# Head sums of an RWKV-7 preparation: one full product or four on the quarters of the array

## The chip, the cores and the metric

The kernel runs on one core of a Trainium2 chip. The metric is the device time of one execution in microseconds (us). The engines are called as in the profile: PE is TensorE (matmuls), PEld its weight loads, DVE VectorE, ACT ScalarE, POOL GpSimd, SP the queue that issues most DMAs. PE writes its results into eight PSUM banks of 128 partitions by 512 fp32 numbers.

## The reference

One decoder block on 512 tokens with a model width of 1024: a norm, one input projection, two mixers (sparse attention and RWKV-7), gates, an output projection, then a gated MLP with a short convolution. The change lies in the preparation of the RWKV-7 mixer, which has eight heads of 64 channels:

```python
r, k, v, a, decay = heads(r), heads(k), heads(v), heads(a), heads(decay)
kk = k * k_k
kk = kk / jnp.maximum(jnp.sqrt(jnp.sum(kk * kk, axis=-1, keepdims=True)), 1e-12)
k = k * (1.0 + (a - 1.0) * k_a)
...                        # the scan over tokens gives y, which is normalised per head
y = y + jnp.sum(r * k * r_k, axis=-1, keepdims=True) * v
```

Two sums over the 64 channels of a head occur for every token: the one of `kk * kk`, whose inverse root normalises the key, and the one of `r * k * r_k`, which weights the value.

## The kernel before

Activations are held with channels on the 128 partitions and the 512 tokens along the free dimension, so one tile holds two heads (a head pair, p = 0 to 3): head 0 in partitions 0 to 63, head 1 in 64 to 127. A projection (`dense_fm`) makes one such tile of 128 output channels from 24 matmuls of 512 columns: eight with the high part of the weights (`whi`) on each of two parts of the activations (`hh`, `hl`), eight with the low part (`wlo`). `wnext` loads the weights by DMA, one tile ahead of its use, and splits them in two on ACT and DVE.

The stage in question goes over the head pairs. For each, `front` makes the key `kx`, the rate `aa` and the decay (`cl`, `cum`, `ep`, `pi`; two products of 64 rows with `wa`, in banks "a" and "b"), `norms` the inverse root `rn`, `receptance` makes `rx`, `values_of` makes `vx`, `values_tok` turns `vx` to tokens on partitions (four transposes, L545) and copies it into `UV`, `vectors` makes the vectors of the state recurrence in a row of DVE operations and the term `BO`, and `gram` makes the 64x64 chunk matrices `AB` (transposes at L576, then products of 64 rows). The projections of the next pair are written between the steps of this one, so that PE has them while other engines work.

A sum over the channels of a head is a sum over 64 partitions. It is made by PE: `ones` is a 128x128 matrix with ones in two diagonal blocks of 64, and `mm(ss, ones, kk, True, True)` puts into all 64 partitions of a head the sum of that head, for 512 tokens. An fp32 product is carried out in two passes.

Order: in this stage it isn't written out by hand. Each engine's queue is in an order that the compiler's scheduler makes from the program's order (as priority), from dependencies and from its own estimate of times; `tc.high_priority()` raises a block's priority. Engines work through their queues in order. Later stages fix PE's order by hand (`manual_schedule`). PSUM banks come in three groups: "mm" (4 banks, for projections), "a" (2, from `pa()`) and "b" (2, from `pb()`). A new tile of a group waits until the oldest is read out. After the last pair, DVE inverts triangular blocks of `AB` in 31 steps, while PE does the projections of the attention.

Of the kernel before, what the change touches and what calls it, by code (L numbers as in the profile page):

```python
# [13 lines left out]
AF = mybir.ActivationFunctionType  # L14
ALU = mybir.AluOpType
# [8 lines left out]
DH = 64  # L24
H = 8
NH2 = H // 2
# [54 lines left out]
def hybrid_block(ctx: ExitStack, tc: tile.TileContext, A: dict, out: bass.AP):  # L81
# [25 lines left out]
    def bank(tag, bufs, shape=(128, 512)):  # L107
        return ps.tile(list(shape), F32, name="ps_" + tag, tag=tag, bufs=bufs)

    def mmb():  # L110
        return bank("mm", 4)

    def pa():
        return bank("a", 2)

    def pb():
        return bank("b", 2)

    def mm(o, l, r, start, stop):
        te.matmul(o, lhsT=l, rhs=r, start=start, stop=stop)  # L120

    def act(o, i, f=AF.Copy, **kw):
        sc.activation(o, i, f, **kw)  # L123

    def tt(o, a, b, op):
        v.tensor_tensor(o, a, b, op=op)  # L126

    def ts(o, a, s1, s2, op0=ALU.mult, op1=ALU.add):
        if s2 is None:
            v.tensor_scalar(o, a, s1, None, op0=op0)  # L130
        else:
            v.tensor_scalar(o, a, s1, s2, op0=op0, op1=op1)

    def stt(o, a, s, b, op0=ALU.mult, op1=ALU.add):
        v.scalar_tensor_tensor(o, a, s, b, op0=op0, op1=op1)  # L135
# [3 lines left out]
    ident, mask, ones, cmask = kc[:, 0:128], kc[:, 128:256], kc[:, 256:384], kc[:, 384:416]  # L139
# [16 lines left out]
    for name in ("rwkv_mu", "rwkv_w0", "rwkv_a0", "rwkv_k_k", "rwkv_k_a", "rwkv_r_k", "rwkv_ln_g", "rwkv_ln_b"):  # L156
        r0, n = ROWS[name]
        src = A[name]
        if name == "rwkv_r_k":
            src = src.rearrange("l h d -> l (h d)")  # L160
# [3 lines left out]
    pt = pa()  # L164
# [3 lines left out]
    def col(name, i=0):  # L168
        r0, n = ROWS[name]
        return prm[:, r0 + i:r0 + i + 1]  # L170
# [37 lines left out]
    def norm_tiles(pool_):  # L208
        return (cp.tile([128, NT, 2], F32, name="ss", tag="ss"),
                [pool_.tile([128, D], F32, name="h", tag="h", bufs=NT) for _ in range(NT)])  # L210
# [123 lines left out]
    with tc.manual_schedule(engines={getattr(mybir.EngineType, e) for e in ("PE", "Activation", "DVE", "Pool")}):  # L334
# [37 lines left out]
        for k in range(KT):  # L372
# [5 lines left out]
            if k == 6:  # L378
                pt = pa()
# [37 lines left out]
    def dense_fm(xh, xl, kt=KT):  # L417
        return run(dense_fm_g(xh, xl, kt))
# [12 lines left out]
    UV = rp.tile([128, NCH, NH2, 2, DH], F32, name="UV")  # L431
    BO = gp.tile([128, 4, S], F32, name="BO", tag="BO")
# [11 lines left out]
    def shift_mix(p, m, dst):  # L444
        mu = col("rwkv_mu", m)
        act(dst, p, AF.Copy, scale=omm[:, m:m + 1])
        stt(dst[:, 1:], p[:, :-1], mu, dst[:, 1:])

    def t2(name, bufs=1):
        return tp.tile([128, S], F32, name=name, tag=name, bufs=bufs)  # L450
# [11 lines left out]
    for name, (r0, n) in ROWS.items():  # L462
        if r0 >= NR0:
            r0 -= NR0
            src = A[name]
            if name.startswith("cmp_pe"):
                src = src.rearrange("l a d -> l (a d)")
# [10 lines left out]
    def chunks(ap):  # L478
        return ap.rearrange("p (c t) -> p c t", t=C)
# [15 lines left out]
    def front(p):  # L495
        cs = slice(128 * p, 128 * p + 128)
        kx = t2("kx", 2)
        pk = dense_fm(hh, hl)
        zw, za = pa(), pb()
        mm(zw, wa[0:64, cs], xw[0:64], True, True)  # L500
        mm(za, wa[64:128, cs], xw[64:128], True, True)
        shift_mix(pk, 4 + p, kx)
        cl = t2("cl")
        act(cl, zw, AF.Tanh, scale=0.5, bias=w0h[:, p:p + 1])
        aa = t2("aa", 2)
        act(aa, za, AF.Tanh, scale=0.5, bias=a0h[:, p:p + 1])
        ts(cl, cl, -0.5 * DECAY, -0.5 * DECAY)
        cum = t2("cum")
        v.tensor_tensor_scan(out=cum, data0=scanm.rearrange("p c t -> p (c t)"), data1=cl, initial=0.0,
                             op0=ALU.mult, op1=ALU.add)  # L510
        ep = tp.tile([128, NCH, C + 1], F32, name="ep", tag="ep", bufs=2)
        v.memset(ep[:, :, 0:1], 1.0)
        act(ep[:, :, 1:], chunks(cum), AF.Exp)
        pi = t2("pi", 2)
        act(pi, cum, AF.Exp, scale=-1.0)
        v.tensor_copy(PC[:, p, :, None], ep[:, :, C:C + 1])
        L[p] = dict(kx=kx, aa=aa, ep=ep, pi=pi)

    def norms(p):
        kx = L[p]["kx"]  # L520
        kk = t2("kk", 2)
        act(kk, kx, AF.Square, scale=col("rwkv_k_k", p))
        ss = pa()
        mm(ss, ones, kk, True, True)
        rn = t2("rn", 2)
        ts(rn, ss, 1e-24, None, op0=ALU.max)
        act(rn, rn, AF.Ln)
        act(rn, rn, AF.Exp, scale=-0.5)
        L[p].update(kk=kk, rn=rn)

    def receptance(p):
        rx = t2("rx", 2)
        shift_mix(dense_fm(hh, hl), p, rx)
        L[p]["rx"] = rx

    def values_of(p):
        vx = t2("vx")
        shift_mix(dense_fm(hh, hl), 8 + p, vx)
        L[p]["vx"] = vx

    def values_tok(p):
        vx = L[p]["vx"]
        pt = pb()
        for i in range(4):
            te.transpose(pt[:, 128 * i:128 * i + 128], vx[:, 128 * i:128 * i + 128], ident)  # L545
        for r in range(2):
            for cc in range(2):
                act(UV[64 - 64 * r:128 - 64 * r, cc::2, p, r, :],
                    pt[64 * cc:64 * cc + 64].rearrange("p (c r d) -> p c r d", r=2, d=DH)[:, :, r, :])

    def vectors(p):
        kx, aa, ep, pi, kk, rn, rx, vx = (L[p][k] for k in ("kx", "aa", "ep", "pi", "kk", "rn", "rx", "vx"))
        stt(AR[:, p, :, 1, :], chunks(rx), 1.0, ep[:, :, 1:], ALU.mult, ALU.mult)
        stt(kk, kx, col("rwkv_k_k", p), rn, ALU.mult, ALU.mult)
        stt(AR[:, p, :, 0, :], chunks(kk), -1.0, ep[:, :, 0:C], ALU.mult, ALU.mult)
        stt(kk, aa, 1.0, kk, ALU.add, ALU.mult)
        bh = tp.tile([128, NCH, 3, C], F32, name="bh", tag="bh")
        stt(bh[:, :, 0, :], chunks(kk), 0.5, chunks(pi), ALU.mult, ALU.mult)
        v.tensor_copy(bh[64:128, :, 2, :], bh[64:128, :, 0, :])
        ts(aa, aa, kah[:, p:p + 1], oma[:, p:p + 1])  # L560
        stt(kx, kx, 1.0, aa, ALU.mult, ALU.mult)
        stt(bh[:, :, 1, :], chunks(kx), 1.0, chunks(pi), ALU.mult, ALU.mult)
        tv = t2("tv")
        stt(tv, rx, col("rwkv_r_k", p), kx, ALU.mult, ALU.mult)
        L[p]["bh"] = bh
        bs = pa()
        mm(bs, ones, tv, True, True)
        tt(BO[:, p], bs, vx, ALU.mult)

    def gram(p):  # L570
        bh = L[p]["bh"]
        ptr = [pb(), pa()]
        for c in range(NCH):
            for r in range(2):
                rs = slice(64 * r, 64 * r + 64)
                te.transpose(ptr[r][:, 64 * c:64 * c + 64], bh[rs, c, r:r + 2].rearrange("p a t -> p (a t)"),  # L576
                             ident[rs, rs])
        for r in range(2):
            act(BKT[:, :, p, r, :], ptr[r].rearrange("p (c j) -> p c j", c=NCH))
        for c0 in range(0, NCH, 4):  # L580
            ptr = [mmb(), mmb()] if c0 else [pb(), pa()]
            for i in range(4):
                for r in range(2):
                    rs = slice(64 * r, 64 * r + 64)
                    mm(ptr[r][:, 128 * i:128 * i + 128], bh[rs, c0 + i, r:r + 2].rearrange("p a t -> p (a t)"),
                       AR[rs, p, c0 + i].rearrange("p a t -> p (a t)"), True, True)
            for r in range(2):
                tt(AB[:, c0:c0 + 4, p, r, :], ptr[r].rearrange("p (c t) -> p c t", c=4),
                   mask[:, None, :].to_broadcast([128, 4, 128]), ALU.mult)


    front(0)
    norms(0)
    receptance(0)
    values_of(0)
    late_params()
    for p in range(NH2):
        if p + 1 < NH2:
            front(p + 1)
            norms(p + 1)  # L600
        values_tok(p)
        vectors(p)
        if p + 1 < NH2:
            receptance(p + 1)
        gram(p)
        if p + 1 < NH2:
            values_of(p + 1)
        if p + 2 == NH2:
            kcp = dense_fm(hh, hl)
# [15 lines left out]
    for g in range(2):  # L625
        for b in range(2):
            r = 64 * g + 32 * b
# [75 lines left out]
    pt = pa()  # L703
# [31 lines left out]
    for b in (1, 0):  # L735
        for g in range(2):
            r = 64 * g + 32 * b
# [511 lines left out]
    for m in range(KT):  # L1249
        cs = slice(128 * m, 128 * m + 128)  # L1250
# [13 lines left out]
    ss, hs = norm_tiles(ntp)  # L1264
# [36 lines left out]
    with tc.manual_schedule(engines=KTS):  # L1301
        for t in range(NT):
            qs = slice(128 * t, 128 * t + 128)
            p = mmb()
# [13 lines left out]
        for pair in range(2):  # L1318
            cs = slice(256 * pair, 256 * pair + 256)
# [37 lines left out]
    for hf in range(2):  # L1357
        bo = dense_tok(512, aT[:, 0], aT[:, 1], NF)
        for t in range(NT):
            n = 256 if hf and t == NT - 1 else 512  # L1360
            for c0 in range(0, 512, n):
                cs = slice(512 * hf + c0, 512 * hf + c0 + n)
# [30 lines left out]
```

## Time and profile before

| | |
|---|---|
| median of 3 runs | 837.78 us (837.58 to 837.99) |
| the profiled execution | 837.93 us |
| its span, from the first to the last instruction | 836.1 us |
| granted clock of PE | 1.00 |
| the stage from front(0) to gram(3) | about 30 to 123 us of the span |

Times in the timelines count from the start of the span. A row gives start and duration in us, engine, line and operation; a line can be that of a helper: L120 is `mm`, L123 `act`, L126 `tt`, L130 and L132 `ts`, L135 `stt`, L299 the low part of a weight split. "x4" is a number of like instructions, and what stands in brackets is idle time of the engine before, and what ended it. A row of the groups gives after the count the busy us, the mean ns of one, and idle time before. PE's matmuls are pipelined, so their recorded durations overlap.

### The profile page before, as it was taken

What the parts mean: (1) busy time and instruction counts of PE and PEld (TensorE: products, weight loads), DVE (VectorE), ACT (ScalarE), POOL (GpSimd) and SP (SyncE); (2) the same over time, 40 slices, a digit from 0 to 9 for tenths busy, and PEclk for the clock granted to TensorE, in tenths of its full rate; (3) what the DMA queues carried; (4) which work ended last, traced back from release to release, by engine and by line L of the source; (5) the groups of instructions that cost most, each with busy time, mean ns of one, the idle gap of its engine ahead of it and who ended that gap; (6) DMA issues with size and microseconds to landing.
All of it is one profiled execution on the core that took longest, in us unless ns stands there. A gap on an engine that the chain in (4) does not pass through costs nothing.

```text
span 836.1 us, 12860 instructions
## 1 busy us (share of the span) xinstructions
PE 822.2 (98%) x5097; PEld 667.1 (80%) x5097; DVE 514.2 (62%) x998; ACT 406.7 (49%) x792; POOL 52.4 (6%) x69
## 2 busy tenths in 40 slices
PE   7999999999999999999999999999999999999998
PEld 5777778887787876777788988888888888888886
DVE  4478779973565778787664665666555666322222
ACT  6766654463555777676334454444444444221210
POOL 5200020140000100111000000000000000000000
PEclk9999999999999999999999999999999999999999
DMA  7432222346452310000275033332333332223421
GB/s 228 116 78 75 76 76 77 72 125 182 116 114 77 83 45 13 26 26 26 64 249 179 1 101 100 101 99 87 93 101 101 100 101 91 88 100 114 139 75 51
DMA packets 109104, 78.73 MB, mean 94 GB/s; under 512 B 3869, under 2 KB 97748, under 8 KB 109044
## 3 DMA queue, kind: packets, MB, share of 16 engines
q1 hardware_dynamic: 106512, 73.51, 30.4%
q10 hardware_dynamic: 1060, 2.55, 1.0%
q0 software_dynamic: 1472, 1.86, 1.0%
q8 instruction: 40, 0.66, 0.3%
q14 instruction: 20, 0.16, 0.1%
HBM read 74.56 MB, written 2.29 MB: 92 GB/s over the span
## 4 chain that ended last, share of the span: by engine, by line
PE 53%; DVE 0%; DVEq 0%; issue 0%
PE ps_mm L120 52%; PE ps_a L203 0%; PE ps_b L203 0%; PE ps_a L120 0%; PE ps_b L1197 0%; PE ps_mm L1197 0%; DVE x L126 0%; DVEq L1389 0%; PE ps_a L1149 0%
## 5 line engine op out<-in xcount | busy, mean ns | idle before, releaser
L299 DVE TENSOR_TENSOR wlo<-raw,whi 128x1024 fp32r<-128x1024 f32 (+1 forms) x111 | 131.5, 1186 | 184.8 <-PE ps_mm L120 157.2
L120 PE MATMUL ps_mm<-hh,whi 128*128 128x512 f32 (+1 forms) x624 | 242.6, 391 | 0.6 <-ACT whi L123 0.5
L120 PE MATMUL ps_mm<-hl,whi 128*128 128x512 f32 (+1 forms) x624 | 240.4, 387 | 0.0
L123 ACT ACTIVATE whi<-raw 128x1024 fp32r<-128x1024 f32 (+3 forms) x124 | 123.3, 996 | 165.2 <-PE ps_mm L120 143.9
L120 PE MATMUL ps_mm<-hh,wlo 128*128 128x512 f32 (+1 forms) x624 | 151.7, 384 | 0.0
L120 PEld LDWEIGHTS ps_mm<-hh,whi 128*128 128x128 f32 x624 | 117.3, 188 | 27.3 <-issue 1.3
L120 PEld LDWEIGHTS ps_mm<-hl,whi 128*128 128x128 f32 x624 | 117.4, 188 | 23.4 <-issue 1.0
L120 PEld LDWEIGHTS ps_mm<-hh,wlo 128*128 128x128 f32 x624 | 115.1, 188 | 23.3
L120 PE MATMUL ps_mm<-whi,aT 128*128 128x512 f32 x352 | 84.5, 390 | 0.0
L120 PEld LDWEIGHTS ps_mm<-whi,aT 128*128 128x128 f32 x352 | 65.9, 188 | 14.3 <-issue 0.4
L135 DVE SCALAR_TENSOR_TENSOR cgv<-ps_mm,cw,cgv 128x511 f32<-128x511 f32 (+1 forms) x88 | 65.4, 746 | 1.6
L123 ACT ACTIVATE cgv<-ps_mm,cw 128x512 f32<-128x512 f32 x44 | 34.2, 779 | 23.3 <-PE ps_mm L120 23.3
L120 PE MATMUL ps_mm<-wlo,aT 128*128 128x512 f32 x176 | 44.3, 389 | 0.0
L123 ACT ACTIVATE P<-P,nm 128x512 f32<-128x512 f32 (+3 forms) x64 | 35.3, 553 | 14.9 <-DVE nm L1171 14.9
L123 ACT ACTIVATE aT<-cgv 128x512 fp32r<-128x512 f32 x22 | 13.9, 632 | 56.8 <-DVE cgv L126 56.8
L120 PEld LDWEIGHTS ps_mm<-wlo,aT 128*128 128x128 f32 x176 | 33.0, 188 | 6.9
L123 ACT ACTIVATE cgv<-cgv 128x512 f32<-128x512 f32 x22 | 13.9, 632 | 41.0 <-DVE cgv L135 41.0
L299 POOL TENSOR_TENSOR wlo<-raw,whi 128x512 fp32r<-128x512 f32 (+3 forms) x13 | 20.5, 1573 | 202.2 <-PE ps_mm L120 148.2
L1171 DVE CUSTOM_DVE_ANT_0 P<-ps_a,AB 128x512 f32<-128x512 f32 (+3 forms) x64 | 29.4, 485 | 4.2 <-PE ps_a L120 3.7
L126 DVE TENSOR_TENSOR x<-x,ps_mm 128x512 f32<-128x512 f32 (+1 forms) x17 | 11.1, 655 | 23.6 <-PE ps_mm L120 22.0
L126 DVE TENSOR_TENSOR aT<-cgv,aT 128x512 fp32r<-128x512 f32 x22 | 15.2, 693 | 14.7 <-ACT aT L123 14.7
L120 PE MATMUL ps_a<-KH,qst 128*128 128x512 f32 (+3 forms) x64 | 21.3, 348 | 1.6 <-DVE nm L1171 0.9
(358 smaller groups left out, 1199.1 us busy)
## 6 DMA issues: line engine op xcount, KB each, us to landing
raw<-in_w_up_dram SPq DMA_DIRECT2D x44, 512.0 KB, 3.8
raw<-in_w_in_dram SPq DMA_DIRECT2D x38, 512.0 KB, 3.9
raw<-in_w_down_dram SPq DMA_DIRECT2D x22, 512.0 KB, 3.6
raw<-in_w_out_dram SPq DMA_DIRECT2D x8, 512.0 KB, 3.5
xt<-in_x_dram SPq DMA_DIRECT2D x4, 512.0 KB, 5.9
raw<-in_cmp_w_v_dram SPq DMA_DIRECT2D x4, 512.0 KB, 3.8
raw<-in_w_proj_b_dram SPq DMA_DIRECT2D x8, 256.0 KB, 2.7
raw<-in_w_proj_a_dram SPq DMA_DIRECT2D x8, 256.0 KB, 2.7
```

What stands on the lines that cost most here:

```text
L120: te.matmul(o, lhsT=l, rhs=r, start=start, stop=stop)
L123: sc.activation(o, i, f, **kw)
L126: v.tensor_tensor(o, a, b, op=op)
L135: v.scalar_tensor_tensor(o, a, s, b, op0=op0, op1=op1)
L299: eng.tensor_tensor(lo, raw, hi.bitcast(F32), op=ALU.subtract)
L1171: v.tensor_tensor_reduce(out=P[:, i], in0=sp[:, N * (i - i0):N * (i - i0) + N], in1=BT[:, h, 384 - 128 * qt:512], scale=-1.0, scalar=-NEG, ...
```

## The change

A head sum becomes four products of 64x64 with 256 tokens each (`head_sums`). For the first 256 tokens head 0's rows go to partitions 0 to 63 and head 1's to 64 to 127, into a bank "a"; for the other 256 tokens they go crosswise, into a bank "b". The four thus use the four quarters of the array, with two banks of which half is filled. What is read from bank "b" has its heads exchanged: `EXCH` lists the three pieces (the first 256 tokens whole, the others in two halves of 64 partitions), and the last step behind each sum undoes it, an Exp in three parts in `norms`, a multiplication in three parts in `vectors`. The clamp of `norms` is made in two parts and, like Ln, in `kk` in place of `rn`. Besides, `values_tok(p)` is written ahead of `norms(p + 1)`, and its four copies into `UV` get high priority.

```diff
+    def head_sums(src):
+        o = [pa(), pb()]
+        for i in range(2):
+            for r in range(2):
+                a, b = slice(64 * r, 64 * r + 64), slice(64 * (r ^ i), 64 * (r ^ i) + 64)
+                mm(o[i][b, 0:256], ones[a, a], src[a, 256 * i:256 * i + 256], True, True)
+        return o
+
+    EXCH = [(slice(0, 128), slice(0, 128), 0), (slice(0, 64), slice(64, 128), 1), (slice(64, 128), slice(0, 64), 1)]
+
     def norms(p):
         kx = L[p]["kx"]
         kk = t2("kk", 2)
         act(kk, kx, AF.Square, scale=col("rwkv_k_k", p))
-        ss = pa()
-        mm(ss, ones, kk, True, True)
+        ss = head_sums(kk)
         rn = t2("rn", 2)
-        ts(rn, ss, 1e-24, None, op0=ALU.max)
-        act(rn, rn, AF.Ln)
-        act(rn, rn, AF.Exp, scale=-0.5)
+        for i in range(2):
+            ts(kk[:, 256 * i:256 * i + 256], ss[i][:, 0:256], 1e-24, None, op0=ALU.max)
+        act(kk, kk, AF.Ln)
+        for d, s_, i in EXCH:
+            cs = slice(256 * i, 256 * i + 256)
+            act(rn[d, cs], kk[s_, cs], AF.Exp, scale=-0.5)
...
-        for r in range(2):
-            for cc in range(2):
-                act(UV[64 - 64 * r:128 - 64 * r, cc::2, p, r, :],
-                    pt[64 * cc:64 * cc + 64].rearrange("p (c r d) -> p c r d", r=2, d=DH)[:, :, r, :])
+        with tc.high_priority():
+            for r in range(2):
+                for cc in range(2):
+                    act(UV[64 - 64 * r:128 - 64 * r, cc::2, p, r, :],
+                        pt[64 * cc:64 * cc + 64].rearrange("p (c r d) -> p c r d", r=2, d=DH)[:, :, r, :])
...
-        bs = pa()
-        mm(bs, ones, tv, True, True)
-        tt(BO[:, p], bs, vx, ALU.mult)
+        bs = head_sums(tv)
+        for d, s_, i in EXCH:
+            cs = slice(256 * i, 256 * i + 256)
+            tt(BO[d, p, cs], bs[i][s_, 0:256], vx[d, cs], ALU.mult)
...
         if p + 1 < NH2:
             front(p + 1)
+        values_tok(p)
+        if p + 1 < NH2:
             norms(p + 1)
-        values_tok(p)
         vectors(p)
```

## The prediction

> **What bounds the kernel now.** I read the page first, then busy time by stretches over the stage that the change touches (from 30 us, front(0), to 123 us, the end of gram(3)), then the timelines of each engine there.
>
> ```profile
> span 836.1 us, 12860 instructions
> PE 822.2 (98%) x5097; PEld 667.1 (80%) x5097; DVE 514.2 (62%) x998; ACT 406.7 (49%) x792; POOL 52.4 (6%) x69
> ```
>
> The profiled execution took 837.93 us, so 1.83 us lie around its span; the median of the runs is 837.78, or 0.15 lower. TensorE (PE) is busy for 98% of the span, so time is won by taking work from PE, if no new wait takes its place, and lost by any stop of PE. Where a wait could come from shows in the stretches of one head pair. Their columns are busy us (instructions) of PE, weight loads, DVE, ACT and POOL:
>
> ```profile
> 74.60:85.00 10.40, 10.40 (x81) 8.03 (x82) 5.24 (x8) 10.00 (x16) 0.00 (x0) 1.00 0.36 99
> 85.00:95.40 10.40, 10.40 (x47) 8.58 (x48) 10.24 (x16) 3.79 (x5) 0.00 (x0) 1.00 0.18 51
> 97.08:107.50 10.42, 10.42 (x81) 8.05 (x82) 5.24 (x8) 10.03 (x16) 0.00 (x0) 1.00 0.36 101
> 107.51:118.67 11.16, 10.96 (x48) 8.71 (x47) 11.03 (x17) 3.76 (x5) 0.06 (x1) 1.00 0.13 45
> ```
>
> The averages (62% and 49%) hide this: in the first half of each period of 22.5 us ACT is 96% busy (from cl of front to rx of receptance), in the second DVE is 98 to 99% busy (from rx to vx of values_of). The two halves form one chain, cl to rx on ACT and then rx to vx on DVE, and its end is awaited by the four transposes at L545. How much room it has:
>
> ```profile
> 95.44 0.74 DVE L135 SCALAR_TENSOR_TENSOR vx<-ps_mm,prm,vx 128x511 f32<-128x511 f32 x1
> 96.98 0.66 PE L545 MATMUL ps_b<-kc,vx 128*128 128x128 f32 x4
> ...
> 117.93 0.74 DVE L135 SCALAR_TENSOR_TENSOR vx<-ps_mm,prm,vx 128x511 f32<-128x511 f32 x1
> 118.73 0.66 PE L545 MATMUL ps_b<-kc,vx 128*128 128x128 f32 x4 [0.26 <-DVE vx L135]
> ```
>
> For head pair 2 vx ends at 96.18, 0.80 us before PE comes to it. For head pair 3 there is no next front to cover it, and PE already waits: DVE sets the time there.
>
> **Head sums on PE.** Eight products are replaced: kk and tv, four times each. In the timeline of PE (start, duration, operation), the two of period 2:
>
> ```profile
> 99.56 1.02 PE L120 MATMUL ps_a<-kk,kc 128*128 128x512 f32 x2
> 100.42 1.02 PE L120 MATMUL ps_a<-tv,kc 128*128 128x512 f32 x2
> 100.88 0.79 PE L120 MATMUL ps_mm<-hl,whi 128*128 128x512 f32 x1
> 101.51 0.40 PE L120 MATMUL ps_mm<-hh,whi 128*128 128x512 f32 x1
> ```
>
> Durations include the latency of the pipeline, so I go by starts. From kk to tv are 0.86 us: two passes of 512 columns at 0.43. A dense matmul takes 0.226 (below), so the one before 101.51 took the array at 101.28, and tv also cost 0.86: a full product costs nothing for coming and going. The new form is four 64x64 products of 256 columns on the four quarters, two passes of 0.215 each. That four quarters with different streams do run together, the state loop shows, with U and the next chunk's own products on four quarters and two banks:
>
> ```profile
> 185.27 0.81 PE L120 MATMUL ps_mm<-wlo,hh 128*128 128x280 f32 x5
> 186.01 0.27 PE L120 MATMUL ps_b<-Xs,AB 64*64 64x64 f32 x2
> 186.03 0.27 PE L120 MATMUL ps_b<-UV,AB 64*64 64x64 f32 x2
> ...
> 186.48 0.23 PE L120 MATMUL ps_b<-UV,AB 64*64 64x64 f32 x2
> 186.64 0.40 PE L120 MATMUL ps_mm<-whi,hh 128*128 128x280 f32 x1
> 186.87 0.30 PE L120 MATMUL ps_mm<-whi,hl 128*128 128x280 f32 x1
> ```
>
> Two groups of two start 0.02 apart, and eight such steps are 0.064 apart, where 64 columns alone would be 0.43/8 = 0.054. But the block as a whole is dearer. The five before it step by (0.81 - 0.29)/4 = 0.13 and end their stream at 185.92; the dense work is back in step at 186.87 - 0.13 = 186.74. Of those 0.82 us the steps are 0.51; 0.31 goes to entering and leaving. The same from the pair of front, half the rows each:
>
> ```profile
> 29.62 1.97 PE L120 MATMUL ps_mm<-hh,wlo 128*128 128x512 f32 x8
> 31.53 0.69 PE L120 MATMUL ps_a<-xw,wa 64*128 64x512 f32 x1
> ...
> 32.06 0.59 PE L120 MATMUL ps_a<-xw,wa 64*128 64x512 f32 x1
> ...
> 32.59 0.50 PE L120 MATMUL ps_mm<-hh,whi 128*128 128x512 f32 x1
> 32.92 0.39 PE L120 MATMUL ps_mm<-hl,whi 128*128 128x512 f32 x1
> ```
>
> Dense steps are (1.97 - 0.39)/7 = 0.226, so the stream ends at 31.43 and is back at 32.69: 1.26 us for two passes of 0.43, 0.40 for the switch. I take 0.36, midway. The Trainium skill differs within itself here: TensorE: Matmul & The Clock Gate, Part 3, counts for a pack of small products the span of one plus some 4 ns for each further one and nothing for the switch, by which a head sum would cost 0.44 (an estimate) and the eight would win 3.4 us; TensorEngine Tiling, Key Properties, says that changing the tiling mode drains the engine. Both blocks here are with the second.
>
> A head sum by itself then costs 0.43 + 0.36 = 0.79 against 0.86: 0.07 won. Two in a row share the switch: 0.86 + 0.36 = 1.22 against 1.72, 0.50 won. In three periods kk of the next pair and tv of this one do stand together, as above, and I expect that to stay: they take their banks in the same order, and the transposed values are out of their bank earlier. Together: 0.07 for kk of pair 0, 3 x 0.50, and for tv of pair 3, which goes on to gram's own small products and pays one side only, 0.86 - 0.43 - 0.18 = 0.25. PE work falls by 1.8 us. If the order puts dense matmuls between the two, 0.36 is lost each time.
>
> **What it adds on ACT and DVE.** Half-width operations are dearer than half:
>
> ```profile
> L123 ACT ACTIVATE rn<-rn 128x512 f32<-128x512 f32 x8 | 5.1, 632 | 0.1
> L123 ACT ACTIVATE QK<-ps_mm 64x256 f32<-64x256 f32 x8 | 3.0, 376 | 0.7 <-PE ps_mm L120 0.6
> L126 DVE TENSOR_TENSOR BO<-ps_a,vx 128x512 f32<-128x512 f32 x4 | 2.8, 692 | 2.1 <-PE ps_a L120 2.1
> L126 DVE TENSOR_TENSOR sC<-sC,mx 128x256 f32<-128x256 f32 x8 | 3.4, 420 | 0.0
> ```
>
> The last Exp becomes three of about 0.376: 1.13 for 0.63, +0.50 in each period, in ACT's full half and ahead of rx in its queue. The clamp becomes two of 0.42 for one like BO's 0.69 (+0.15), BO three for one (+0.57); both fall in the half in which DVE is busy 5.2 of 10.4 us and cost nothing while it has those 5 us. Ln stays whole. The matrix `ones`, the tiles and every DMA stay as they are; no queue of SP or POOL is touched.
>
> The order of values_tok and norms(p+1) changes little on PE, where the transposes came first already (96.98 before 99.56). The high priority does change ACT: the four evacuations move ahead of aa and the square of kk, which wait for them.
>
> ```profile
> 98.24 0.72 ACT L123 ACTIVATE kk<-kx,prm 128x512 f32<-128x512 f32 x1
> ...
> 102.90 1.99 PE L120 MATMUL ps_mm<-hh,wlo 128*128 128x512 f32 x8
> ...
> 119.42 1.54 ACT L123 ACTIVATE UV<-ps_b 64x256 f32<-64x256 f32 x4 [1.66 <-PE ps_b L545]
> ```
>
> They take 1.54 us, so the square ends near 100.5 instead of 98.96, and the head sums move later inside the dense product of receptance, which runs until 104.7 (the eight of its last part, from 102.90) and covers that. ACT's sum of work is the same, as long as Ln finds its clamp done: the chain grows by the 0.50 alone. Bounds: 0 (if Exp is queued behind rx) and 2.0 (if the 1.54 comes back as idle ACT).
>
> **Where it comes due.** With PE 0.50 shorter and the chain 0.50 longer a period, the room of 0.80 for L545 becomes -0.2 in periods 1 and 2: a small stop each. Up to front(3) PE is ahead by 0.07 + 0.50 + 0.50 - 0.2 = 0.87; vx of pair 3 comes 0.87 - 0.50 = 0.37 earlier, and the third pair's 0.50 is spent waiting for it. Then the tail of pair 3:
>
> ```profile
> 119.22 1.02 PE L120 MATMUL ps_a<-tv,kc 128*128 128x512 f32 x2
> 120.17 0.27 PE L576 MATMUL ps_b<-kc,bh 64*128 64x64 f32 x1
> 120.28 0.69 DVE L126 TENSOR_TENSOR BO<-ps_a,vx 128x512 f32<-128x512 f32 x1 [1.61 <-PE ps_a L120]
> 121.02 0.37 PE L120 MATMUL ps_b<-AR,bh 64*128 64x128 f32 x1
> ```
>
> There are two "b" banks. Before, the transposed values held one and gram's transposes (L576) took the other at 120.17; gram's products then waited until the evacuation ended at 119.42 + 1.54 = 120.96. Now tv's sum holds the second, and L576 itself must wait for that evacuation (or for BO's third part, 0.2 later). The 0.6 us of L576, hidden in that wait before, come behind it. Sum at gram(3): -0.37 + 0.6 = +0.2 us. After it PE works through in step, and DVE's inverse starts from the same point. So 837.93 + 0.2 = 838.1 for a profiled execution, 838.0 as median: no change that can be told (0.2%, 1.7 us, is about what a measurement of this kernel can tell).
>
> **Rivals.** Two of them rest on these rows:
>
> ```profile
> 35.95 0.68 DVE L130 TENSOR_SCALAR rn<-ps_a 128x512 f32<-128x512 f32 x1
> 36.37 1.28 ACT L123 ACT_TABLE_LOAD   x1
> ...
> 113.07 0.69 ACT L123 ACTIVATE vx<-ps_mm,omm 128x512 f32<-128x512 f32 x1 [0.75 <-PE ps_mm L120]
> ```
>
> (1) The gain comes through, 0.20: the DVE queue gets vx of pair 3 before tv's work, or L576 finds a bank. Then all 1.8 us are won, 836.1. For: the input of vx was ready at 113.76, four us before DVE came to it at 117.93, and any new order may move it. Against: it stood last in each of the periods before.
>
> (2) The quarters switch for free, 0.08: 8 x (0.86 - 0.43) = 3.4 us, 834.4, if order and waits allow it. Against are the two switch prices above, 0.31 and 0.40, and the chain. It is the time that the rule of the Trainium skill's TensorE: Matmul & The Clock Gate, Part 3, above would give.
>
> (3) Slower, 0.25: ACT's half becomes the period. Place: Ln, behind clamp, sum and square, all pushed back 1.54 us by the evacuations; the chain grows by 2.0 instead of 0.5. It decides from 0.3 of growth a period (0.80 - 0.50 of PE's lead). L545 then stops PE for 2.0 - 0.3 = 1.7 once before front(3); lag there -1.07 + 1.7 = +0.6, vx at +2.6, tail +0.6: +3.2, 841. For: ACT has 0.4 us idle in that half. Against: Ln has a table load ahead of it that does not wait for its clamp (36.37, while the clamp ran until 36.63), 1.28 us of ACT work that takes up most of the 1.54. The Trainium skill (TensorEngine Tiling, PSUM Bottleneck) warns that tiling leaves PSUM evacuation as it was, which is this case.
>
> (4) The change doesn't do what it says, 0.02: the quarters run one after another, 8 x (1.72 + 0.36 - 0.86) less three shared switches, +8.7, 846.6. The state loop's rows speak against it.
>
> **How the numbers follow.** The forecast has 0.45. Faster by over 0.2% (below 836.1): rival 2, 0.12 of rival 1, whose price lies at that edge, and 0.04 of the forecast's scatter from a new order, 0.24. Slower (above 839.5): 0.22 of rival 3, rival 4 and 0.06 of scatter, 0.30. The range reaches down to rival 1 and up almost to rival 3's price: 836.0 to 840.8.
>
> **What would show it.** Right: pairs of four-quarter head sums of about 1.2 us from dense to dense, PE waiting on vx at L545 and on UV at L576 of pair 3, PE busy near 821. Wrong: head sums that cost 0.5 each, dense matmuls between kk's and tv's quarters, vx of pair 3 well before PE needs it, or PE stopped for over a microsecond a period at L545.

## The result

The changed kernel takes 839.68 us (median of 10 runs, 839.29 to 841.28) against 837.84 before (10 runs, 837.50 to 838.32). The ratio is 1.0025, with a 95% interval of 1.0016 to 1.0035: slower by 1.8 us, inside the predicted range and just past the 0.2% up to which the prediction spoke of no change. By the prediction's own line of 839.5 this is the slower outcome, which it gave 0.30; its centre, 838.0, was missed by 1.7. The page after (busy time, share of the span, instructions):

```profile
span 837.6 us, 12983 instructions
...
PE 821.5 (98%) x5145; PEld 667.0 (80%) x5145; DVE 516.8 (62%) x1010; ACT 409.9 (49%) x800; POOL 52.8 (6%) x69
```

PE is busy 0.7 us less, but the span is 1.5 us longer. The waits of PE from 28 to 126 us of the span (sum, times, longest) say why:

```profile
PE ps_b L559 <- DVE vx L135: 2.0, 3, 1.3
PE ps_a L120 <- ACT kk L123: 1.0, 3, 0.7
PE ps_b L592 <- ACT UV L123: 0.5, 1, 0.5
PE ps_mm L120 <- DVE AB L126: 0.2, 1, 0.2
```

L559 and L592 are L545 and L576 of before. The same view of before has 0.3 us for `vx` and 0.2 for `AB`, 0.5 in all; now it is 3.7. In PE's timeline (start, duration, what the idle time before waited for):

```profile
57.25 0.43 PE L120 MATMUL ps_a<-kk,kc 64*64 64x256 f32 x2 [0.69 <-ACT kk L123]
...
74.65 0.66 PE L559 MATMUL ps_b<-kc,vx 128*128 128x128 f32 x4 [0.31 <-DVE vx L135]
...
119.82 0.66 PE L559 MATMUL ps_b<-kc,vx 128*128 128x128 f32 x4 [1.34 <-DVE vx L135]
...
122.12 0.46 PE L592 MATMUL ps_b<-kc,bh 64*128 64x64 f32 x4 [0.53 <-ACT UV L123]
```

The last pair's transposes come at 119.82 instead of 118.73. The last 16 Gram products (`ps_mm<-AR`) come at 123.54 instead of 122.01, and that difference of 1.53 is the difference of the spans: the stages behind it are as long as before.

The stretches of the last period, cut as in the prediction (from the transposes to `rx`, from `rx` to the next transposes; columns as there):

```profile
97.24:106.55 9.31, 9.13 (x82) 6.99 (x84) 6.62 (x11) 7.82 (x14) 0.00 (x0) 1.00 0.42 113
106.56:119.82 13.26, 11.92 (x64) 9.55 (x60) 11.21 (x17) 6.42 (x9) 1.20 (x1) 1.00 0.14 41
```

DVE's half was 11.16 us long and 99% busy; now it is 13.26 us long and 85% busy (11.21 / 13.26). DVE has hardly more to do in it (11.21 us against 11.03); it stands still. Its timeline shows where:

```profile
106.56 0.75 DVE L135 SCALAR_TENSOR_TENSOR rx<-ps_mm,prm,rx 128x511 f32<-128x511 f32 x1 [0.15 <-ACT rx L123]
109.14 0.75 DVE L135 SCALAR_TENSOR_TENSOR kk<-kx,prm,rn 128x512 f32<-128x512 f32 x1 [1.84 <-ACT rn L123]
109.81 0.69 DVE L135 SCALAR_TENSOR_TENSOR AR<-rx,ep 128x512 f32<-128x512 f32 x1
...
119.03 0.74 DVE L135 SCALAR_TENSOR_TENSOR vx<-ps_mm,prm,vx 128x511 f32<-128x511 f32 x1
```

The normalised key waits 1.84 us for the inverse norm `rn`, and AR's receptance part and the masked Gram blocks, which need no `rn`, stand behind it in the queue. Before, in the same place:

```profile
107.51 0.75 DVE L135 SCALAR_TENSOR_TENSOR rx<-ps_mm,prm,rx 128x511 f32<-128x511 f32 x1 [1.31 <-ACT rx L123]
108.18 0.74 DVE L135 SCALAR_TENSOR_TENSOR kk<-kx,prm,rn 128x512 f32<-128x512 f32 x1
```

There the key followed `rx` at once. Why `rn` is late, ACT's timeline shows, first before, then after:

```profile
101.95 1.28 ACT L123 ACT_TABLE_LOAD   x1
103.24 0.63 ACT L123 ACTIVATE rn<-rn 128x512 f32<-128x512 f32 x1
...
106.13 0.63 ACT L123 ACTIVATE rn<-rn 128x512 f32<-128x512 f32 x1
```

```profile
101.66 0.71 ACT L123 ACTIVATE kk<-kx,prm 128x512 f32<-128x512 f32 x1
...
104.02 1.28 ACT L123 ACT_TABLE_LOAD   x1 [0.71 <-DVE kk L130]
105.31 0.63 ACT L123 ACTIVATE kk<-kk 128x512 f32<-128x512 f32 x1
...
107.83 1.27 ACT L123 ACTIVATE rn<-kk 128x256 f32<-128x256 f32 x3
```

The square starts at 101.66 (before: 98.24), the load of Ln's table now waits for the clamp, and Exp in three takes twice as long: `rn` is complete at 109.10 instead of 106.76.

### The profile page after: what moved, and what is told of

Same layout as the page of the kernel before. It is cut to its first block, busy times and chain, and to the rows that moved or that the text cites. A ratio compares the mean times of both kernels' runs of the same rounds, so it can differ in the third digit from the quotient of the medians.

```text
span 837.6 us, 12983 instructions
## 1 busy us (share of the span) xinstructions
PE 821.5 (98%) x5145; PEld 667.0 (80%) x5145; DVE 516.8 (62%) x1010; ACT 409.9 (49%) x800; POOL 52.8 (6%) x69
## 4 chain that ended last, share of the span: by engine, by line
PE 53%; DVE 0%; DVEq 0%; issue 0%
PE ps_mm L120 52%; PE ps_b L203 0%; PE ps_a L203 0%; PE ps_a L120 0%; PE ps_b L1214 0%; PE ps_mm L1214 0%; DVE x L126 0%; DVEq L1406 0%; PE ps_a L1166 0%
```

## The experiments

Each ratio is taken against the kernel before, timed beside the run; its medians there were 837.68 (first four), 837.92 (next four), 837.75 (next three) and 837.83 (last).

### Order and priority alone (e1)

```diff
 kernel before, head sums as full products
+        with tc.high_priority():
             for r in range(2): ... act(UV[...], pt[...])
...
+        values_tok(p)
         if p + 1 < NH2:
             norms(p + 1)
-        values_tok(p)
```

> The kernel before with only the order of the change: values_tok ahead of norms, its four copies into UV at high priority, head sums as full products. Theory A (the change loses because the copies push the square of kk, and with it the chain from cl over Ln, Exp, rx and DVE to vx, back by about a microsecond a period): slower than before by 0.4 to 1.2 us, about 838.6, with PE waiting at the value transposes of pair 3 for 0.8 us or more (before 0.26). Theory B (the loss comes from the quarters: switches on PE and half-width work on ACT and DVE): as before, 837.8.

Measured: 837.55 us, ratio 0.9998 (0.9989 to 1.0006). PE's waits in the stage are one line:

```profile
PE ps_mm L120 <- DVE AB L126: 0.2, 1, 0.2
```

The reordering costs nothing. It also took away the 0.3 us of waiting for `vx`. The loss comes with the quarters. The late square alone is not the cause either: here too it starts at 100.90 instead of 98.24. But Ln's table load ran from 102.57, ahead of the clamp at 102.82, and Ln followed it at 103.86.

### The quarters alone (e2), and the change without the priority (e3)

```diff
 e2: changed kernel
-        with tc.high_priority():
-            ... act(UV[...])
+        ... act(UV[...])
-        values_tok(p)
         if p + 1 < NH2:
             norms(p + 1)
+        values_tok(p)
 e3: only the first of the two
```

> The changed kernel with norms ahead of values_tok as before and without the high priority: only the head sums on the quarters are left of the change. Theory A: the square is not pushed back, the chain grows only by the split Exp; between 837.3 and 838.3, about 837.8. Theory B: the loss stays, 839.5 or so.

> The changed kernel without the high priority on the four copies; values_tok still stands ahead of norms. Theory A, if the priority is what pushes the square back: 838.2 or so. Theory A, if the place in the program does it already (program order is priority): as changed, 839.5. Theory B: as changed, 839.7.

Measured: e2 844.04 us, ratio 1.0074 (1.0061 to 1.0086); e3 842.64, ratio 1.0055 (1.0043 to 1.0068). Both are slower than either theory had said. In e2 PE waited for a bank of group "b":

```profile
PE ps_b L120 <- ACT UV L123: 4.2, 3, 1.4
```

So the order and the priority do not pay by themselves, but the quarters need them: without both, the copies into `UV` keep a "b" bank for which the Gram products then wait. For e3 this reason is not shown. Its runs scatter from 841.11 to 843.93, and in the execution that was profiled (841.19) PE waited for `vx` (2.4 us) and for `kk` (2.3), and for the copies into `UV` only 0.5.

### Another bank for the last pair (e4)

```diff
-    def head_sums(src):
-        o = [pa(), pb()]
+    def head_sums(src, bank_b=pb):
+        o = [pa(), bank_b()]
...
-        bs = head_sums(tv)
+        bs = head_sums(tv, pb if p + 1 < NH2 else mmb)
```

> The changed kernel with one difference: the crosswise half of the last pair's value sum goes to a bank of the projections' group instead of group b, so that gram's transposes of pair 3 find a bank. The prediction's tail term (0.6 us for a bank that is not free) says 0.4 to 0.6 us faster than the changed kernel, 839.2, and no wait of those transposes for the copies. If the tail costs nothing: 839.7.

Measured: 839.02 us, ratio 1.0014 (1.0005 to 1.0023). That is 0.66 less than the changed kernel, or 0.50 if each is taken against the kernel before timed beside it (+1.34 against +1.84). From the last pair's transposes to the last 16 Gram products it was 3.29 us, as before (3.28), instead of 3.72. That is the tail that the prediction put at 0.6.

### Which side of the change (e5, e6)

```diff
 e5: changed kernel, sum of kk as before
-        ss = head_sums(kk)
+        ss = pa()
+        mm(ss, ones, kk, True, True)
         ... clamp, Ln and Exp on rn, whole, as before
 e6: changed kernel, sum of tv as before
-        bs = head_sums(tv)
+        bs = pa()
+        mm(bs, ones, tv, True, True)
         ... BO in one, as before
```

> The changed kernel with its order and priority, but the sum of kk is again one full product with one clamp and one Exp; only tv's sum is on quarters. Theory K (the loss sits on kk's side: clamp and Exp in parts, inverse norms late, so the chain front to vx grows by 1.24 us a period and the transposes wait 2.0 us in three periods): the chain falls back, the waits at the transposes go, 837.6 to 838.6 us against 839.7 of the changed kernel, although the products alone cost PE 0.86 + 0.79 instead of 1.22 us in three periods (+1.3). Theory T (the loss sits on tv's side: the second bank of group b taken between the transposes of vx and the Gram step, BO in three pieces on DVE): waits stay and the PE work grows, 839.5 to 841.

> The changed kernel with its order and priority, but the sum of tv is again one full product and one BO product; only kk's sum is on quarters. Theory K: the inverse norms stay late, the transposes still wait for vx in every period, 839.2 to 840.3 us. Theory T: the bank is free for the Gram step and DVE has 0.57 us less a period, so the waits go and PE pays +1.3 us for two single sums instead of a pair: 838.0 to 838.8.

Measured: e5 839.78 us, ratio 1.0024 (1.0014 to 1.0033); e6 838.25, ratio 1.0002 (0.9993 to 1.0011). By the numbers that is theory T, but the traces give another reason for either. In e5 PE waits for neither `vx` nor `kk`; its periods are longer (73.92 to 97.12 from front to front, 23.20 us, against 22.48 before), since the order pulled one head sum apart:

```profile
54.13 0.39 PE L120 MATMUL ps_mm<-hh,whi 128*128 128x512 f32 x1
54.45 0.65 PE L120 MATMUL ps_b<-tv,kc 64*64 64x256 f32 x4
55.03 0.50 PE L120 MATMUL ps_mm<-hl,whi 128*128 128x512 f32 x1
55.36 0.39 PE L120 MATMUL ps_mm<-hh,whi 128*128 128x512 f32 x1
```

Its crosswise half alone costs 0.77 us: dense work ends at 54.13 + 0.23 = 54.36 and is back in step at 55.36 - 0.23 = 55.13. Two of the quarters are filled, for the full 0.43, and 0.34 is the switch; the other half pays 0.78 more at 57.93. So e5 prices a sum pulled apart and does not answer its question. As for the chain it agrees with theory K: from front(3) to the end of `vx` it is 23.00 us (22.74 before, 23.98 in the changed kernel). That no transposes wait says less, since the longer period gives them 0.72 us more room.

In e6 the chain got shorter, 22.74 us, although the inverse norm is made as in the changed kernel. DVE's timeline:

```profile
106.92 0.69 DVE L135 SCALAR_TENSOR_TENSOR AR<-rx,ep 128x512 f32<-128x512 f32 x1
108.72 0.75 DVE L135 SCALAR_TENSOR_TENSOR kk<-kx,prm,rn 128x512 f32<-128x512 f32 x1 [1.11 <-ACT rn L123]
```

The scheduler here put AR's receptance part ahead of the key that waits for `rn`, and the idle time fell from 1.84 to 1.11; PE's waits at L559 fell from 2.0 to 0.3 us. Of the 1.24 us by which the chain is shorter, 0.61 lie behind the start of `rx`; by the other 0.63 `rx` itself is earlier, as the transposes ahead of the `UV` copies no longer come late. This pointed to the place in DVE's queue, which e10 tests.

### The square first (e7), the values earlier (e8)

```diff
 e7: changed kernel
-        act(kk, kx, AF.Square, scale=col("rwkv_k_k", p))
+        with tc.high_priority():
+            act(kk, kx, AF.Square, scale=col("rwkv_k_k", p))
 e8: changed kernel
-        gram(p)
         if p + 1 < NH2:
             values_of(p + 1)
+        gram(p)
```

> The changed kernel with high priority on the square of kk too: ACT then does it ahead of the four UV copies, and the Exp in three ahead of the evacuation of receptance. Theory K: the 1.84 us that DVE waits for the inverse norm in every period goes, vx is 1.0 to 1.8 us earlier and no transposes wait for it: 838.0 to 838.8 us. Rival (the growth is ACT's own work, not its order): what is gained at the inverse norms is lost at the UV copies and the receptance, each later by 0.7 to 1.3 us, and PE waits at other instructions: 839.3 to 841.

> The changed kernel with the values of the next pair written ahead of the Gram step, so that vx is no longer the last thing that the next transposes wait for. If the price of the change is only the wait at the transposes (2.0 us in three periods), it goes: 837.7 to 838.3 us. If the chain is ACT's and DVE's work in sum, PE waits as long at another instruction of the period (the Gram products, banks of group b): 839.4 to 840.2.

Measured: e7 842.60 us, ratio 1.0054 (1.0041 to 1.0068); e8 840.24, ratio 1.0029 (1.0017 to 1.0040). e7 is slower than both of its theories had said, e8 is where its second one had it. In e7 the idle time for `rn` was gone, as theory K had it. But the square came so early that kk's crosswise half had to wait for a "b" bank (the `UV` copies ended at 79.74), and PE did its two sums in pieces, with a dense product between them:

```profile
78.63 0.65 PE L120 MATMUL ps_a<-kk,kc 64*64 64x256 f32 x4
79.11 0.60 PE L120 MATMUL ps_a<-tv,kc 64*64 64x256 f32 x4
79.80 0.65 PE L120 MATMUL ps_b<-kk,kc 64*64 64x256 f32 x4
80.38 0.50 PE L120 MATMUL ps_mm<-hl,whi 128*128 128x512 f32 x1
80.81 0.65 PE L120 MATMUL ps_b<-tv,kc 64*64 64x256 f32 x4
```

PE was busy 825.1 us instead of 821.5. In e8 no transposes wait for `vx`, and one other instruction waits as long:

```profile
PE ps_a L592 <- DVE bh L574: 2.3, 1, 2.3
```

That looks like the second theory, but DVE's and POOL's timelines give another reason:

```profile
119.23 2.46 DVE L574 COPY bh<-bh 64x512 f32<-64x512 f32 x1
```

```profile
118.62 2.79 POOL L299 TENSOR_TENSOR wlo<-raw,whi 128x1024 fp32r<-128x1024 f32 x1 [90.96 <-PE ps_mm L120]
```

The copy took 0.42 us for the other three pairs and for all pairs of the changed kernel; here it fell beside a weight split on POOL and took 2.46. That the split slowed it was not tested apart. Without these 2.04 us the time would be about 838.2 us (an estimate), as the first theory has it: what PE would wait for next, the copies into `UV`, ends at 118.95 + 1.55 = 120.50, and PE came on at 121.84. So e8 doesn't tell the two theories apart. It leaves it open that an early `vx` alone, with the key still waiting 1.84 us in three periods, would win most of the loss back.

### Exp in one piece (e9), the receptance part first (e10)

```diff
 e9: changed kernel, the clamp undoes the exchange
-        for i in range(2):
-            ts(kk[:, 256 * i:256 * i + 256], ss[i][:, 0:256], 1e-24, None, op0=ALU.max)
-        act(kk, kk, AF.Ln)
         for d, s_, i in EXCH:
             cs = slice(256 * i, 256 * i + 256)
-            act(rn[d, cs], kk[s_, cs], AF.Exp, scale=-0.5)
+            ts(rn[d, cs], ss[i][s_, 0:256], 1e-24, None, op0=ALU.max)
+        act(rn, rn, AF.Ln)
+        act(rn, rn, AF.Exp, scale=-0.5)
 e10: changed kernel
         stt(AR[:, p, :, 1, :], chunks(rx), 1.0, ep[:, :, 1:], ALU.mult, ALU.mult)
-        stt(kk, kx, col("rwkv_k_k", p), rn, ALU.mult, ALU.mult)
+        kc1 = tp.tile([128, 1], F32, name="kc1", tag="kc1", bufs=2)
+        stt(kc1, AR[:, p, 0, 1, 0:1], 0.0, col("rwkv_k_k", p), ALU.mult, ALU.add)
+        stt(kk, kx, kc1, rn, ALU.mult, ALU.mult)
```

> The changed kernel with the exchange of halves done by the clamp on DVE (three pieces into rn) instead of by the Exp on ACT, so that Ln and Exp are one instruction each, as before the change. Theory X (the chain that sets the transposes runs clamp, Ln, Exp in three, normalised key): ACT's part of the chain falls by 0.67 us a period and DVE's clamp grows by some 0.4, so the last vx is 0.3 to 0.7 us earlier and the time 839.0 to 839.4 against 839.7. Rival (the chain runs through DVE's queue alone): the clamp's 0.4 is added and nothing is gained, 839.7 to 840.5.

> The changed kernel with the receptance part of AR (0.69 us on DVE) forced ahead of the normalised key: the key's scalar is copied in one DVE instruction of one column that depends on AR, nothing else is altered. In the changed kernel DVE stands idle 1.84 us a period for the inverse norm with that AR part queued behind the waiting instruction; in the version with tv as a full product it stood ahead and the wait was 1.11. Theory Q (place in the queue): idle falls to 0 to 1.1 us a period, vx of the last pair comes 0.6 to 1.5 us earlier, the transposes' 2.0 us of waiting falls below 0.8: 838.2 to 839.0. Rival (the idle is no loss, since something else feeds vx): same waits, 839.6 to 840.2.

Measured: e9 837.71 us, ratio 0.9999 (0.9990 to 1.0008); e10 837.22, ratio 0.9994 (0.9984 to 1.0003). Both win more than either theory had said. For e10, DVE's timeline in the last period:

```profile
106.08 0.75 DVE L135 SCALAR_TENSOR_TENSOR rx<-ps_mm,prm,rx 128x511 f32<-128x511 f32 x1 [0.15 <-ACT rx L123]
106.87 0.69 DVE L135 SCALAR_TENSOR_TENSOR AR<-rx,ep 128x512 f32<-128x512 f32 x1
107.48 0.68 DVE L126 TENSOR_TENSOR AB<-ps_b,kc 128x512 f32<-128x512 f32 x1
...
108.68 0.15 DVE L135 SCALAR_TENSOR_TENSOR kc<-AR,prm 128x1 f32<-128x1 f32 x1
108.94 0.75 DVE L135 SCALAR_TENSOR_TENSOR kk<-kx,kc,rn 128x512 f32<-128x512 f32 x1
...
116.36 0.74 DVE L135 SCALAR_TENSOR_TENSOR vx<-ps_mm,prm,vx 128x511 f32<-128x511 f32 x1
117.02 0.74 DVE L135 SCALAR_TENSOR_TENSOR tv<-rx,prm,kx 128x512 f32<-128x512 f32 x1
```

AR's part and two Gram blocks now fill the time until `rn` is there (108.64), and nothing waits. From the start of `rx` to the end of `vx` it is 11.02 us instead of 13.21 (119.77 - 106.56). Not all of that is the one move: the scheduler answered by putting `vx` ahead of `tv`, which brings `vx` another 0.67 us. The move of the key would have been just enough for the last transposes, which start at 117.83: with `tv` first `vx` would have ended at 117.10 + 0.67 = 117.77. An instruction of 0.15 us that computes nothing new gives back 2.5 us, more than the whole loss.

In e9 `rn` was ready 4.48 us after the clamp's start instead of 5.91, and only 0.64 of these 1.43 us are the Exp. ACT's timeline has the rest:

```profile
102.11 1.28 ACT L123 ACT_TABLE_LOAD   x1
103.41 0.63 ACT L123 ACTIVATE rn<-rn 128x512 f32<-128x512 f32 x1
```

The clamps of e9 ran from 102.07 to 103.37, so the table was loaded beside them and Ln started when they ended. In the changed kernel the load started 0.08 us after the second clamp's end. So e9 altered two things at once. The traces agree on this: where the clamp writes `kk` (the changed kernel, e3, e4, e6, e8, e10, e12) the load starts 0.08 to 0.09 us behind its end; where it writes `rn` (before, e1, e5, e9, e11) the load does not wait for it. In the last period of e2 and e7, which write `kk`, the clamp was done before ACT came to the load. The built programs of the changed kernel and of e9 show the difference: Ln on `kk` waits for ACT's own earlier instruction, and the wait for DVE is an instruction of its own ahead of the table load; Ln on `rn` carries the wait for DVE itself. The Trainium skill (ScalarE: Activation LUTs, "What ACT_TABLE_LOAD costs") gives about 1283 ns for the load, which these rows confirm, and some 1380 ns of drain on top, of which nothing is seen here: in e9 the load starts 0.02 us after the end of the activation before it (102.09), and Ln starts 0.01 to 0.02 us after the load's end.

### Together (e11, e12)

```diff
 e11: e9 + e10 + e4
 e12: e10 for p > 0 alone, + e4
+        sk = col("rwkv_k_k", p)
+        if p:
+            sk = tp.tile([128, 1], F32, name="kc1", tag="kc1", bufs=2)
+            stt(sk, AR[:, p, 0, 1, 0:1], 0.0, col("rwkv_k_k", p), ALU.mult, ALU.add)
+        stt(kk, kx, sk, rn, ALU.mult, ALU.mult)
```

> The changed kernel with one Exp, the receptance part of AR first, and the last pair's crosswise sum in a bank of group mm. If the three losses (Exp in three, queue place, last bank) are the whole price and the quarters' products gain what the PE rows say (1.8 us), no instruction of PE waits for vx or UV and the time is 835.9 to 837.2 against 837.7 of before. Rival (the chain of ACT and DVE is still the longer side): 838.0 to 838.8.

> The changed kernel with the receptance part of AR ahead of the normalised key for pairs 1 to 3 only (for pair 0, where nothing waits for the inverse norm, the order of the changed kernel stays), and the last pair's crosswise sum in a bank of group mm; Exp in three as in the changed kernel. With that forcing for all pairs PE still waited 1.4 us for the first square and 0.5 for the last UV copies, at 837.2. If those waits add up: the first falls to 0.7 and the second goes, 835.9 to 836.7 us, faster than before (837.75) by 1.0 to 1.9. Rival (PE is no longer what the chain ends on, so less waiting shows elsewhere): 836.9 to 837.6.

Measured: e11 837.37 us, ratio 0.9995 (0.9986 to 1.0003), between the two expectations: the gains don't add up. The exchange in the clamp makes DVE 0.55 us later with BO, whose bank the Gram products need, in e9 already:

```profile
104.75 0.37 PE L120 MATMUL ps_b<-AR,bh 64*128 64x128 f32 x1 [0.28 <-DVE BO L126]
```

From the last transpose before it (104.25) to this product are 0.50 us, where e12 has 0.06, so the stop costs more than its 0.28 us of idle time. With it, e9 and e11 have periods of 22.4 to 22.7 us, no better than before. e12, without that part, took 836.23 us (11 runs, 835.98 to 836.67), ratio 0.9981 (0.9972 to 0.9990): 1.6 us faster than before and 3.45 faster than the change as it was made (before stood at 837.84 there and at 837.83 here). That is what the first expectation said, though the wait for the last `UV` copies did not go. What PE still waits for in the stage:

```profile
PE ps_a L120 <- ACT kk L123: 0.7, 1, 0.7
PE ps_b L120 <- ACT UV L123: 0.4, 1, 0.4
PE ps_mm L120 <- DVE AB L126: 0.2, 1, 0.2
```

And one whole period without a wait, with the pair of head sums in the next:

```profile
73.58 0.69 PE L120 MATMUL ps_a<-xw,wa 64*128 64x512 f32 x1
...
95.54 0.69 PE L120 MATMUL ps_a<-xw,wa 64*128 64x512 f32 x1
...
100.78 0.84 PE L120 MATMUL ps_mm<-hh,wlo 128*128 128x512 f32 x3
101.55 0.43 PE L120 MATMUL ps_a<-kk,kc 64*64 64x256 f32 x2
...
102.57 1.43 PE L120 MATMUL ps_mm<-hh,wlo 128*128 128x512 f32 x5
```

The period is 21.96 us; before it was 73.45 to 95.93, or 22.48. The period ahead of it, in which PE waits 0.7 us for `kk`, is 22.71 us long.

## Why the prediction came out as it did

**The PE terms were right.** Forecast were 1.22 us for two adjacent head sums and 0.50 won a period. The pair of e12 takes the array from 100.78 + 3 x 0.226 = 101.46 to 102.71 (five dense products take 1.29, here 1.43, so they are in step from 102.57 + 0.14): 1.25 us. A period without waits is 0.52 shorter. The switch price of 0.36 a visit held (1.25 - 0.86 = 0.39 here, 0.34 in e5). The Trainium skill's TensorEngine Tiling (Array Packing), Key Properties, which has a change of tiling mode drain the engine, agrees; rival 2, the free switch, fell. Rival 4 fell too: the quarters ran together.

**The step that failed** is "ACT's sum of work is the same, as long as Ln finds its clamp done: the chain grows by the 0.50 alone". From front(3) to the end of `vx` of pair 3 it was 22.74 us before and is 23.98: +1.24, between the bounds of 0 and 2.0 that the prediction gave. In parts, counted from front(3) (95.93 before, 95.79 after):

- The table load of Ln starts at 8.23 instead of 6.02, 2.21 later. The four `UV` copies pushed the square behind `ep` and `pi` as well, not behind themselves alone: it starts 3.56 us later, where 1.54 were forecast. That alone did no harm: in e1 it starts 2.75 later. But here the load waits for the clamp, which the prediction excluded when it argued against rival 3 ("a table load ahead of it that does not wait for its clamp"): true of before, not of a clamp that is written into `kk`.
- From the load to the end of Exp 0.27 are added: 0.64 for Exp in three (0.50 forecast), less 0.37 because the evacuation of `rx` (0.67) and no longer a weight split (1.04) stands between Ln and Exp.
- `rn` is thus 2.48 later, `rx` 0.81 earlier. By kind the 2.48 are 0.71 of waiting for the clamp, 0.64 for Exp in three, 0.67 for the evacuation of `rx`, which came behind Exp before, and 0.46 of other idle time, 0.29 of it for transposes that come late themselves. The chain no longer runs over `rx` but over `rn`, and DVE's queue, which the prediction did not look into, has nothing else in front. The key starts 1.10 later; from there to `vx` it is 10.63 instead of 10.49.

The range held in part by luck: the growth of 1.24 came over `rn` and DVE's queue, a path that the sum doesn't have, and the bound of 2.0 was made of the 0.50 and the copies' 1.54 alone.

**What followed from it.** PE should have led by 0.87 at front(3); it led by 0.14. It was 0.25 ahead at front(0) already, in a stretch that the change doesn't touch (part of why these two profiles differ by 1.5 us where the medians differ by 1.8), and stopped for 1.18 us (0.69 and 0.18 for `kk`, 0.31 for `vx`) where 0.2 were forecast. The prediction had the dense product of the receptance cover the later head sums; it did not cover them wholly. So `vx` of pair 3 came 1.10 later, not 0.37 earlier. The tail was forecast at +0.6 and measured at +0.44, as only the transposes into bank "b" had to wait. Sum at the last Gram products: +1.10 + 0.44 = +1.5 instead of +0.2.

**The rivals.** Rival 3 had the right place (Ln pushed back, idle ACT) and about half its price; the outcome lies between it and the forecast. Rival 1's condition, `vx` ahead of `tv`'s work, came true in e9 to e12, and its time of 836.1 is what e12 gave, though not by the change as it was made. The counter-check "PE stopped for over a microsecond a period" was met in one period of three (1.34), and it pointed to the right stage.

**What is shown and what is not.** That the queue place costs is shown by e10, which alters nothing else in the source; its 2.5 us contain the move of `vx` ahead of `tv`, whose share was not measured apart. In the last period it is 0.67 of 2.19 us. Whether that move alone, with the key still waiting, would have been enough was not run cleanly: e8, which comes nearest, was spoilt by the slow copy. That the late table load makes up 0.78 of the 1.43 us in e9 (net of e9's longer clamp) is read from rows of a run that altered two things; a clamp into a tile of its own, with Exp in three, was not run.

## What to carry to other kernels

A saving on the engine that bounds the kernel is worth what the chain of the others lets through: list for each engine what is queued behind an instruction that the edit makes wait, and see whether that work could go first. Work on quarters of the array paid here when all four were filled in one visit; a sum that the order pulled apart cost 0.77 + 0.78 = 1.55 us (e5), more than the 0.86 of the full product. And before a step is written in place, look at which waits the instruction behind it then has: one of them may end up on a table load that used to be hidden.

## What the runs showed of the hardware that was not expected

A table load of 1.28 us ran beside the clamp in kernels where Ln had only DVE to wait for, and started 0.08 to 0.09 us behind its end where Ln also waited for ACT's own write. Two quarters of the array took as long as four for the same number of columns: 0.77 us for half a head sum in e5, with the switch, and about 0.86 - 0.09 = 0.77 for a whole one in e6, whose period without waits is 22.39 us instead of 22.48. A DVE copy of 64x512 took 2.46 us instead of 0.42 beside a weight split on POOL (e8).
